# Four-term products of softmax weights and values per head, and earlier reads of weights, in a two-layer attention and expert trunk

## The chip, the cores and the metric

The kernel runs on one core of a Trainium2 chip. The metric is the device time of one execution in microseconds (us), from the runs that were timed; the profile is one further execution.

## The reference

The input is one sequence of 512 tokens of width 1024. Two layers follow each other, and each has a token mixer, a residual sum with layer norm, a feed-forward part of 16 experts of which each token uses two, and a second residual sum with layer norm.

```
for layer in range(2):
    mixed = mixer_dilated(x, ...) if layer == 0 else mixer_stick_breaking(x, ...)
    x = layer_norm(ALPHA * x + mixed, ln1_g[layer], ln1_b[layer])
    ffn = moe_ffn(x, router_w, router_b, exp_w_gate[layer], exp_w_up[layer], exp_w_down[layer])
    x = layer_norm(ALPHA * x + ffn, ln2_g[layer], ln2_b[layer])
```

The mixer of layer 0 projects three groups of queries, keys and values for 16 heads of 64; each group attends with a window and a dilation, `softmax(q k / 8 + bias) v`, and the groups are merged by their softmax denominators. The mixer of layer 1 is a stick-breaking attention with one group of queries, keys and values. All matrix products are wanted at fp32 accuracy.

## The kernel before, in words

**Splitting.** A number is carried as a high and a low part of type fp32r, `hi` (rounded by ACT, line 143) and `lo` (the remainder, by DVE, line 145); the helper is `split`. A product is three matmuls, hi·hi, hi·lo and lo·hi (`mm3`, lines 150 to 153). Weights come as chunks: `load` (line 205) fetches a chunk to `raw`, `split_to` makes `whi` and `wlo`, `weights` hands them out.

**Order.** The program is written as steps that are interleaved by hand (`interleave`, `beside`); a scheduler then orders the instructions of every engine by its own estimate. Each engine and each DMA queue works its list in order.

**Start.** The rows of x are loaded by SP (line 375), transposed by TensorE and split into `xT` (`rows_to_T`, line 324). Two of the four row blocks are transposed ahead of the first projection, the other two inside it (`rest`). `load_router` (line 390) loads the router's weights and the four rows of `ln1_g` and `ln1_b` from ACT's queue, the latter with one element per partition and run (line 400).

**Layer 0's attention** works in quarters of four heads. `project` makes Q, K and V of a unit; the far units (dilated, two groups together) and the near unit of a quarter are attended by `attend` (line 599). For each pair of heads `pr` and each half `b2` of the query blocks it takes a bank `po` from the pool `psD` (two banks), and for each of two blocks `j`: scores `S` (line 619), bias and row extreme on DVE (line 624), exponential on ACT (line 629), transposes (line 634), a split into `Ph` and `Pl` (line 637), and the product with the values, which are kept as `Vh` and `Vl` with the two heads of a pair side by side, 128 columns (line 639). A matmul there has the 128 columns of both heads against the 256 columns of both heads' weights, so half of what it makes is not used. ACT then copies each head's half to `acc` (line 642).

**Layer 1's weights, ahead.** Beside layer 0's projection steps, `split_ahead` (line 269) takes one quarter of a chunk of layer 1's weights: it loads it from HBM to a buffer `raw` (line 274), splits it, and stores the two parts to HBM (`kept`, line 276, POOL's queue). There are 64 such quarters. All use one buffer, which holds the raw quarter and both parts; the next load waits until the store before it has landed. Layer 1 then loads the parts by `parts_of` (line 278); each load is made to wait for the last expert load issued so far (`recent`) and for the last read of layer 0's sum (`read`). `prefetch` (line 900) starts the loads of the layer's first experts during the attention's end.

**Experts.** Each expert's output rows (96 slots, of which some are empty) are added to a DRAM tensor `x2_d` by an indirect DMA (line 1127). Empty slots go to spare rows behind the 512 tokens; those rows are filled first from `xres` (line 1286). At the end `post` sums each token's row: ACT copies both halves with an accumulated sum (line 1268), DVE makes the mean (line 1269), ACT the squares, DVE the scaled rows.

Of the kernel before, what the change touches and what calls it, by code (L numbers as in the profile page):

```python
# [70 lines left out]
def trunk_kernel(ctx, tc, A, out):  # L71
# [133 lines left out]
    def load(i):  # L205

        srcs, kind, j = chunks[i]
        if i in raws or kind == "b":
            return
        k = srcs[0].shape[1]  # L210
        if kind == "a":
            raw = rawp.tile([P, 2048], F32, name="raw0")
            raws[i] = [raw[:, :1024], raw[:, 1024:]]
            for half, t in enumerate(raws[i]):
                load_part(t, srcs, half, 2)
            return
# [155 lines left out]
    for n in range(4):  # L372
        if n == 2:
            load_to(1)
        sp.dma_start(xres[:, n, :], x[n * P:(n + 1) * P, :])

    rest = []
    for n in range(4):
        if n < 2:
            at["begun"] = rows_to_T(*xS, xres[:, n, :], n, streams=True)  # L380
        else:
            rest.append(lambda n=n: rows_to_T(*xS, xres[:, n, :], n, streams=True))
# [7 lines left out]
    def load_router():  # L390
        tmp = xp.tile([P, 5, KT * NE], F32, name="tmp", tag="Ol")
        rw = tmp[:, 0].rearrange("p (k e) -> p k e", k=KT)
        gbs = tmp[:, 1, :4 * KT].rearrange("p (j k) -> p j k", j=4)
        sums = tmp[:, 4, :4 * NE].rearrange("p (j e) -> p j e", j=4)
        with tc.issue_after(at["begun"]):
            act.dma_start(rw, A["router_w"].rearrange("(k p) e -> p k e", p=P))
            act.dma_start(rb, bass.AP(tensor=A["router_b"].tensor, offset=A["router_b"].offset, ap=[[0, P], [1, NE]]))
            for l in range(2):
                for i, name in enumerate(("ln1_g", "ln1_b")):
                    act.dma_start(gbs[:, 2 * l + i], A[name][l].rearrange("(k p) -> p k", p=P))  # L400
        for l in range(2):
            w2 = [rwg[l], tmp[:, 2].rearrange("p (k e) -> p k e", k=KT)]
            for i in range(2):
                tt(w2[i], rw, gbs[:, 2 * l + i, :, None].to_broadcast([P, KT, NE]), op=ALU.mult)
# [95 lines left out]
    def attention0(c, xSh, xSl, project_out):  # L500
# [50 lines left out]
        def project(far, u):  # L551
# [11 lines left out]
            def gen():  # L563
                for ct in range(2):
                    yield from project_T(xSh, xSl, [lambda ps: q_out(ct, ps), lambda ps: k_out(ct, ps)],
                                         "streams" if u == 0 and ct == 0 else None)
                    if ct == 0:
                        V.extend(qk.tile([P, 4, 256], F32R, name=f"V{s}") for s in "hl")
                        if far:
                            yield from project_V(xSh, xSl, *[lambda n2, t=t: t[:, n2 * 2:n2 * 2 + 2] for t in V])  # L570
                        else:
                            yield from project_V_near(V)
            def project_V_near(V):

                w = weights()
                for i in range(2):
                    ps, cs = bank(psA), slice(i * P, (i + 1) * P)
# [761 lines left out]
```

## Time and profile before

| | before |
|---|---|
| median of 3 runs | 1361.58 us (1356.65 to 1364.33) |
| the profiled execution: its time, its span | 1364.12 us, 1362.3 us |
| PE (TensorE) busy | 1247.7 us, 92% |
| weight loads of PE busy | 1022.9 us, 75% |
| DVE busy | 899.1 us, 66% |
| ACT busy | 859.0 us, 63% |
| POOL busy | 203.4 us, 15% |
| mean granted clock of TensorE | 0.954 of full speed |
| DMA | 289.60 MB, mean 213 GB/s |

The span is from the first to the last instruction; 1.8 us of the execution lie around it. A matmul's busy time overlaps that of the next, so the time that a matmul takes from the engine is read from the distance of two starts. The shares are means over stages: layer 0's attention lasts to about 618 us, its experts to about 830, layer 1's attention from about 875 to 1121, its experts to about 1325. A wait is named after what ended last before the instruction started; "issue" is idle time for which the profile shows no other engine.

### The profile page before, as it was taken

To read this page: it belongs to the slowest core of one execution; us is meant where nothing else is said; L and a number is where in the kernel's file an instruction comes from. 1 tells how busy PE (TensorE), PEld (TensorE's weight loads), DVE (VectorE), ACT (ScalarE), POOL (GpSimd) and SP (SyncE) were. 2 spreads that over 40 slices of the span, in tenths; PEclk is the share of its full clock that TensorE was granted. 3 is DMA by queue.
4 is the path that set the end of the run, shared out by engine and by line. 5 is a ranking of instruction groups with operands and counts; after the bars stand their busy time and mean duration, and the time that the engine had idled before them with its cause. 6 is when DMAs were issued, how large, how long until landed. Compare 5 with 4: busy or idle time off the path is not lost. (4 is left out here: it accounts for less than half of the span.)

```text
span 1362.3 us, 19699 instructions
## 1 busy us (share of the span) xinstructions
PE 1247.7 (92%) x6784; PEld 1022.9 (75%) x6784; DVE 899.1 (66%) x1620; ACT 859.0 (63%) x1538; POOL 203.4 (15%) x285
## 2 busy tenths in 40 slices
PE   6999999999999999988799987999999967899876
PEld 5998888789877879877577654988888856677543
DVE  4455665656555645576799774488878857798765
ACT  3356644665356635656699775387778756698664
POOL 3001000011001100010333110022221210332010
PEclk8999999999999999997799999999999977899997
DMA  8865455555455545478699996474444666799982
GB/s 239 284 216 171 155 186 167 178 166 171 147 186 171 164 149 174 158 255 309 226 299 320 312 291 239 132 215 154 156 155 155 218 234 213 249 318 316 288 261 106
DMA packets 176651, 289.60 MB, mean 213 GB/s; under 512 B 17787, under 2 KB 108027, under 8 KB 176540
## 3 DMA queue, kind: packets, MB, share of 16 engines
q1 hardware_dynamic: 153760, 230.72, 51.7%
q0 software_dynamic: 17344, 57.29, 13.5%
q8 instruction: 57, 0.93, 0.3%
q10 hardware_dynamic: 5436, 0.21, 0.3%
q14 instruction: 54, 0.44, 0.1%
HBM read 220.48 MB, written 63.50 MB: 208 GB/s over the span
## 5 line engine op out<-in xcount | busy, mean ns | idle before, releaser
L145 DVE TENSOR_TENSOR wlo<-raw,whi 128x1024 fp32r<-128x1024 f32 x176 | 212.8, 1221 | 94.8 <-ACT whi L143 93.4
L151 PE MATMUL bank<-xTh,whi 128*128 128x512 f32 (+1 forms) x608 | 235.3, 388 | 5.1 <-DVE kl L145 5.1
L152 PE MATMUL bank<-xTl,whi 128*128 128x512 f32 (+1 forms) x608 | 234.2, 385 | 0.0
L153 PE MATMUL bank<-xTh,wlo 128*128 128x512 f32 (+1 forms) x608 | 234.1, 385 | 0.0
L143 ACT ACTIVATE whi<-raw 128x1024 fp32r<-128x1024 f32 x176 | 183.7, 1054 | 67.4 <-PE bank L152 21.1
L145 DVE TENSOR_TENSOR raw<-raw 128x512 fp32r<-128x512 f32 x64 | 44.3, 692 | 141.7 <-ACT raw L143 141.7
L143 ACT ACTIVATE raw<-raw 128x512 fp32r<-128x512 f32 x64 | 40.4, 632 | 152.2 <-DMA raw<-sb_w_in 117.2
L151 PEld LDWEIGHTS bank<-xTh,whi 128*128 128x128 f32 x608 | 116.5, 192 | 24.5 <-issue 5.8
L153 PEld LDWEIGHTS bank<-xTh,wlo 128*128 128x128 f32 x608 | 116.5, 192 | 19.5
L152 PEld LDWEIGHTS bank<-xTl,whi 128*128 128x128 f32 x608 | 117.0, 192 | 18.2
L152 PE MATMUL bank<-wlo,XX 128*96 128x512 f32 x256 | 107.4, 420 | 7.3 <-DVE wlo L145 7.1
L151 PE MATMUL bank<-whi,XX 128*96 128x512 f32 x256 | 106.4, 416 | 7.1 <-ACT whi L143 7.0
L152 PE MATMUL bank<-wlo,xTh 128*128 128x256 f32 x384 | 109.3, 285 | 0.0
L151 PE MATMUL bank<-whi,xTh 128*128 128x256 f32 x384 | 109.1, 284 | 0.0
L153 PE MATMUL bank<-whi,xTl 128*128 128x256 f32 x384 | 109.1, 284 | 0.0
L276 POOL DMA_DIRECT2D kept<-raw x64 | 34.4, 537 | 478.1 <-DVE raw L145 448.5
L153 PE MATMUL bank<-whi,XX 128*96 128x512 f32 x256 | 104.1, 407 | 0.0
L1127 POOL DMA_INDIRECT x_d<-Y,wr x28 | 45.2, 1614 | 201.0 <-ACT Y L1124 139.5
L151 PEld LDWEIGHTS bank<-whi,xTh 128*128 128x128 f32 x384 | 73.7, 192 | 0.5 <-DVE xres L1273 0.2
L152 PEld LDWEIGHTS bank<-wlo,xTh 128*128 128x128 f32 x384 | 73.6, 192 | 0.5
L153 PEld LDWEIGHTS bank<-whi,xTl 128*128 128x128 f32 x384 | 73.3, 191 | 0.1
L629 ACT ACTIVATE Sb<-Sb,st 128x256 f32<-128x256 f32 (+1 forms) x128 | 61.6, 485 | 11.4 <-DVE st L624 11.2
(261 smaller groups left out, 2997.8 us busy)
## 6 DMA issues: line engine op xcount, KB each, us to landing
kept<-raw POOLq DMA_DIRECT2D x64, 512.0 KB, 3.1
raw<-dil_w_in SPq DMA_DIRECT2D x96, 256.0 KB, 4.5
raw<-exp_w_gate SPq DMA_DIRECT2D x32, 512.0 KB, 6.6
raw<-exp_w_up SPq DMA_DIRECT2D x32, 512.0 KB, 7.6
raw<-exp_w_down SPq DMA_DIRECT2D x16, 1024.0 KB, 8.4
whi<-kept SPq DMA_DIRECT2D x32, 512.0 KB, 5.8
wlo<-kept SPq DMA_DIRECT2D x32, 512.0 KB, 5.0
raw<-dil_w_in SPq DMA_DIRECT2D x24, 512.0 KB, 4.6
```

The source lines that it names most:

```text
L143: ins = act.activation(view(hi), src, AF.Copy, scale=scale).ins
L145: tt(view(lo), src, view(hi).bitcast(F32), op=ALU.subtract)
L151: pe.matmul(ps, lhsT=lh, rhs=rh, start=start, stop=False, **kw)
L152: pe.matmul(ps, lhsT=lh, rhs=rl, start=False, stop=False, **kw)
L153: pe.matmul(ps, lhsT=ll, rhs=rh, start=False, stop=stop, **kw)
L276: pool.dma_start(kept[i][part], raw[:, :1024].rearrange("p (j c) -> p j c", j=2))
L629: act.activation(sb[:, b0:, h, :], sb[:, b0:, h, :], AF.Exp, bias=st[:, n, hh, 0:1], scale=-1.0, accum_out=st[:, n, hh, 1:2])
L1127: pool.indirect_dma_start(out=x2_d[:, :], out_offset=bass.IndirectOffsetOnAxis(ap=row, axis=0), in_=Y, in_offset=None, compute_op=ALU.add)
```

## The change

1. **Values times weights (attend).** V of a unit is kept as one tile in which each head has its 64 high and 64 low columns side by side, and the softmax weights as `PP`, in which each head has 128 high and 128 low columns side by side. One matmul of 128 against 256 columns per head and key block makes all four products, lo·lo among them, which is not used. So there are two matmuls per key block and pair instead of three. Each head has a bank of its own, so a pair takes both banks of `psD`. ACT copies lo·hi to `acc`, and DVE adds hi·lo and hi·hi to it.
2. **Layer 1's weights.** One buffer stays allocated; it has two places for raw quarters. A quarter is loaded while the one before it is split. All loads of the parts wait for what the first of them waits for.
3. **Start.** The first chunk's halves are loaded between the row blocks of x. `ln1_g` and `ln1_b` come as 16 rows of 128 elements each and are transposed by TensorE.
4. **Experts.** Empty slots are dropped by a bounds check; the spare rows are gone.
5. **Closing layer norm.** The second half's sum is made by DVE.

```diff
@@ load, load_part
-    def load(i):
+    def load(i, halves=(0, 1)):
         srcs, kind, j = chunks[i]
-        if i in raws or kind == "b":
+        if kind == "b" or i in raws and 0 in halves:
             return
...
@@ split_ahead
     def split_ahead():
+        if not coming:
+            return
+        if "ahead" not in at:
+            at["ahead"] = rawp.tile([P, 2048], F32, name="raw1")
+            fetch_ahead()
+        raw = at["ahead"]
+        i, part = coming.pop(0)
+        src = raw[:, 1024 + part % 2 * 512:][:, :512]
+        fetch_ahead()
+        split(raw[:, :512].bitcast(F32R), raw[:, 512:1024].bitcast(F32R), src)
+        pool.dma_start(kept[i][part], raw[:, :1024].rearrange("p (j c) -> p j c", j=2))
+
+    def fetch_ahead():
         if coming:
-            i, part = coming.pop(0)
-            raw = rawp.tile([P, 2048], F32, name="raw1")
-            load_part(raw[:, 1024:1536], chunks[i][0], part, 4)
-            split(raw[:, :512].bitcast(F32R), raw[:, 512:1024].bitcast(F32R), raw[:, 1024:1536])
-            pool.dma_start(kept[i][part], raw[:, :1024].rearrange("p (j c) -> p j c", j=2))
+            i, part = coming[0]
+            with tc.issue_after(at["begun"]):
+                load_part(at["ahead"][:, 1024 + part % 2 * 512:][:, :512], chunks[i][0], part, 4)
@@ parts_of
-            for before in (at["recent"][-1], at["read"]):
+            at.setdefault("behind", (at["recent"][-1], at["read"]))
+            for before in at["behind"]:
                 after(ins, before)
@@ start
-        if n == 2:
-            load_to(1)
+        if n in (1, 2):
+            load(0, (n - 1,))
         sp.dma_start(xres[:, n, :], x[n * P:(n + 1) * P, :])
@@ load_router
-            for l in range(2):
-                for i, name in enumerate(("ln1_g", "ln1_b")):
-                    act.dma_start(gbs[:, 2 * l + i], A[name][l].rearrange("(k p) -> p k", p=P))
+            for i, name in enumerate(("ln1_g", "ln1_b")):
+                act.dma_start(rows[2 * KT * i:2 * KT * (i + 1)], A[name].rearrange("l (k p) -> (l k) p", p=P))
+        with tc.issue_after(at["begun"]):
+            gbs = bank(psC)[:, :4 * KT]
+            pe.transpose(gbs, rows, ident[:4 * KT, :4 * KT])
...
@@ attend
-                    po = bank(psD).rearrange("p (j h q) -> p j h q", j=2, h=2)
+                    po = [bank(psD).rearrange("p (j c q) -> p j c q", j=2, c=2) for _ in range(2)]
...
-                        Ph = sm.tile([P, 2, 2, P], F32R, name="Ph")
-                        Pl = sm.tile([P, 2, 2, P], F32R, name="Pl")
-                        split(Ph, Pl, pt[:, b0:], view=lambda t: t[:, b0:])
-                        for kb, (Q, K, (Vh, Vl)), kn in kbs:
-                            mm3(po[:, j], Vh[:, kn, vs], Vl[:, kn, vs], Ph[:, kb], Pl[:, kb], kb == b0, kb == 1)
+                        PP = sm.tile([P, 2, 2, 2, P], F32R, name="PP")
+                        split(PP[:, b0:, :, 0], PP[:, b0:, :, 1], pt[:, b0:])
+                        for h in range(2):
+                            for kb, (Q, K, (V,)), kn in kbs:
+                                pe.matmul(po[h][:, j].rearrange("p c q -> p (c q)"),
+                                          lhsT=V[:, kn, pr, 2 * h:2 * h + 2].rearrange("p s d -> p (s d)"),
+                                          rhs=PP[:, kb, h].rearrange("p c q -> p (c q)"), start=kb == b0, stop=kb == 1)
                     for h in range(2):
-                        s = slice(64 * h, 64 * h + 64)
-                        act.activation(perm(acc[s, pr, :], far)[:, 2 * b2:2 * b2 + 2, :], po[s, :, h, :], AF.Copy)
+                        s, other = slice(64 * h, 64 * h + 64), slice(64 - 64 * h, 128 - 64 * h)
+                        to = perm(acc[s, pr, :], far)[:, 2 * b2:2 * b2 + 2, :]
+                        act.activation(to, po[h][other, :, 0], AF.Copy)
+                        for c in (1, 0):
+                            tt(to, to, po[h][s, :, c], op=ALU.add)
@@ expert_down
-                                in_=Y, in_offset=None, compute_op=ALU.add)
+                                in_=Y, in_offset=None, compute_op=ALU.add, bounds_check=T - 1, oob_is_err=False)
@@ post
-                    for half, cs in enumerate(halves):
-                        act.activation(junk[:, cs], ps[half], AF.Copy, accum_out=st[:, n, half:half + 1])
+                    act.activation(junk[:, halves[0]], ps[0], AF.Copy, accum_out=st[:, n, 0:1])
+                    dve.tensor_reduce(st[:, n, 1:2], ps[1], axis=AX.X, op=ALU.add)
@@ layer
-        x2_d = dram.tile([T + P, D], F32, name=f"x2_d{l}")
-        sp.dma_start(x2_d[T:], xres[:, 0])
+        x2_d = dram.tile([T, D], F32, name=f"x2_d{l}")
```

Where instructions move, three places show it. The first is ACT's list at the program's start; `tmp<-ln_g` and `tmp<-ln_b` are DMAs that ACT issues, `xTh` the high part of x, and `raw_604` or `raw_602` the buffer of `split_ahead`. Before, and then with the change:

```order
L143 ACTIVATE xTh<-bank 128x16x32
L396 DMA tmp<-router_w 128x8x16
L397 DMA rb<-router_b 128x16
L400 DMA tmp<-ln_g 128x8x1
L143 ACTIVATE raw_604<-raw_604 128x512
L400 DMA tmp<-ln_b 128x8x1
L400 DMA tmp<-ln_g 128x8x1
L143 ACTIVATE whi<-raw_208 128x1024
L400 DMA tmp<-ln_b 128x8x1
L143 ACTIVATE xTh<-bank 128x16x32 x2
```

```order
L143 ACTIVATE xTh<-bank 128x16x32 x2
L415 DMA tmp<-router_w 128x8x16
L416 DMA rb<-router_b 128x16
L418 DMA tmp<-ln_g 16x128
L143 ACTIVATE raw_602<-raw_602 128x512
L418 DMA tmp<-ln_b 16x128
L143 ACTIVATE xTh<-bank 128x16x32 x2
```

Two DMAs of 1024 runs each and a split of weights no longer stand ahead of the two copies of `xTh` that end each list.

The second is PE's list at the first product of values and weights of a far unit, in the first quarter; rows of `xTh`, `xTl` are projections of the next unit, `Sb` rows are transposes. Before, and then with the change:

```order
L151 MATMUL bank<-xTh,whi 128x512
L151 MATMUL bank<-Ph,Vh 128x256
L152 MATMUL bank<-xTl,whi 128x512
L153 MATMUL bank<-xTh,wlo 128x512
L151 MATMUL bank<-xTh,whi 128x512
L152 MATMUL bank<-xTl,whi 128x512
L153 MATMUL bank<-xTh,wlo 128x512
L152 MATMUL bank<-Pl,Vh 128x256
L153 MATMUL bank<-Ph,Vl 128x256
L151 MATMUL bank<-Ph,Vh 128x256
L152 MATMUL bank<-Pl,Vh 128x256
L153 MATMUL bank<-Ph,Vl 128x256
```

```order
L151 MATMUL bank<-xTh,whi 128x512
L152 MATMUL bank<-xTl,whi 128x512
L153 MATMUL bank<-xTh,wlo 128x512
L664 MATMUL bank<-PP,V 128x256 x8
L659 MATMUL bank<-ident,Sb 128x128 x5
```

Of the twelve matmuls for the two blocks the first six are shown; there are eight now, and they stand together behind the projection.

The third is SP's list near the end of layer 1's attention; `kept_121` holds the parts of the last output weights, the rows of `exp_w` are the first expert loads. Before, and then with the change:

```order
L227 DMA rmh<-exp_w_down 128x2x1024
L227 DMA rmh<-exp_w_gate 128x1024
L227 DMA rmh<-exp_w_up 128x1024
L227 DMA rml<-exp_w_gate 128x1024
L227 DMA rml<-exp_w_up 128x1024
L227 DMA rml<-exp_w_down 128x2x1024
L281 DMA whi<-kept_121 128x2x512
L281 DMA wlo<-kept_121 128x2x512
```

```order
L294 DMA whi<-kept_121 128x2x512
L294 DMA wlo<-kept_121 128x2x512
L228 DMA raw_11423<-exp_w_gate 128x1024
L228 DMA raw_11423<-exp_w_up 128x1024
L228 DMA rmh<-exp_w_down 128x2x1024
L294 DMA whi<-kept_121 128x2x512
L294 DMA wlo<-kept_121 128x2x512
L228 DMA rmh<-exp_w_gate 128x1024
```

The first half of the parts moved ahead of all the expert loads, the second half ahead of all but three.

## Rows read from the trace of the kernel before


**Rows 1.** Busy time by stretch (us, engine busy, granted clock PEclk, DMA share, GB/s).

```profile
40.00:605.00 565.00, 545.44 (x3193) 474.32 (x3193) 317.24 (x661) 311.19 (x632) 48.93 (x88) 1.00 0.55 178
...
780.00:830.00 50.00, 41.45 (x158) 25.32 (x157) 35.35 (x48) 32.08 (x46) 4.48 (x4) 0.93 0.92 289
```

**Rows 2.** PE's waits from 40 to 605 us: engine, line, releaser, us, times, longest.

```profile
PE bank L151 <- ACT Ph L143: 6.6, 8, 1.6
PE bank L151 <- DVE kl L145: 5.1, 4, 3.0
PE bank L151 <- ACT kh L143: 4.8, 6, 1.1
```

**Rows 3.** PE in order of time, 28 to 31 us: start, us, engine, line.

```profile
28.28 1.97 PE L331 MATMUL bank<-ident,xres 128*128 128x128 f32 x8 [6.63 <-DVE xTl L145]
...
30.68 0.41 PE L151 MATMUL bank<-whi,xTh 128*128 128x256 f32 x1
30.89 0.41 PE L152 MATMUL bank<-wlo,xTh 128*128 128x256 f32 x1
```

**Rows 4.** ACT and its queue, 14 to 27 us, in order of time.

```profile
14.81 2.16 ACTq L400 DMA_DIRECT2D tmp<-ln_b  x1
...
22.71 1.06 ACT L143 ACTIVATE whi<-raw 128x1024 fp32r<-128x1024 f32 x1 [7.29 <-issue]
```

**Rows 5.** Busy time by stretch, two stretches with a lowered granted clock.

```profile
28.00:35.00 7.00, 6.72 (x32) 6.49 (x33) 4.87 (x11) 1.20 (x2) 0.00 (x0) 0.53 0.44 123
...
1094.00:1123.00 29.00, 17.82 (x55) 13.32 (x54) 14.11 (x25) 14.26 (x26) 3.79 (x7) 0.71 0.65 232
```

**Rows 6.** PE in order of time, 565 to 566 us; matmuls of 512 and 256 columns.

```profile
565.50 0.39 PE L153 MATMUL bank<-xTh,wlo 128*128 128x512 f32 x1
565.73 0.40 PE L151 MATMUL bank<-xTh,whi 128*128 128x512 f32 x1
...
566.20 0.28 PE L152 MATMUL bank<-Pl,Vh 128*128 128x256 f32 x1
566.32 0.28 PE L153 MATMUL bank<-Ph,Vl 128*128 128x256 f32 x1
```

**Rows 7.** Groups of instructions: count, busy us, mean ns, idle before.

```profile
L151 PE MATMUL bank<-Ph,Vh 128*128 128x256 f32 x120 | 34.9, 290 | 6.6 <-ACT Ph L143 6.6
...
L151 PEld LDWEIGHTS bank<-Ph,Vh 128*128 128x128 f32 x120 | 22.5, 188 | 11.0 <-ACT Ph L143 9.9
```

**Rows 8.** ACT's waits for the next layer's weight pieces, whole run.

```profile
ACT raw L143 <- DMA raw<-sb_w_in: 117.2, 44, 5.6
...
ACT raw L143 <- DMA raw<-sb_w_out: 35.0, 16, 4.7
```

**Rows 9.** One such piece on POOL, SP and ACT, in order of time.

```profile
490.24 0.53 POOL L276 DMA_DIRECT2D kept<-raw  x1 [6.93 <-DVE raw L145]
...
494.84 0.88 SPq L242 DMA_DIRECT2D raw<-sb_w_in  x2
...
497.62 0.63 ACT L143 ACTIVATE raw<-raw 128x512 fp32r<-128x512 f32 x1 [3.53 <-DMA raw<-sb_w_in]
```

**Rows 10.** SP's queue and PE near the second attention's last output weights.

```profile
1088.42 0.38 SPq L227 DMA_DIRECT2D rml<-exp_w_down  x1
...
1094.23 0.38 SPq L281 DMA_DIRECT2D whi<-kept  x1
...
1098.08 0.93 PE L151 MATMUL bank<-whi,Oh 128*128 128x512 f32 x3 [3.81 <-DMA whi<-kept]
```

**Rows 11.** DVE in order of time: contiguous and strided operands read from PSUM.

```profile
602.73 0.42 DVE L145 TENSOR_TENSOR Pl<-bank,Ph 128x256 fp32r<-128x256 f32 x1
...
561.54 1.09 DVE L145 TENSOR_TENSOR kl<-bank,kh 64x512 fp32r<-64x512 f32 x1 [0.42 <-ACT kh L143]
```

**Rows 12.** Groups of instructions: the experts' scatter-adds; the closing layer norm's first pass.

```profile
L1127 POOL DMA_INDIRECT x_d<-Y,wr x28 | 45.2, 1614 | 201.0 <-ACT Y L1124 139.5 <-ACT hh L143 22.5 <-ACT whi L143 15.3
...
L1268 ACT ACTIVATE junk<-bank 128x512 bf16<-128x512 f32 x16 | 9.4, 592 | 8.5 <-SPq L1241 4.3 <-PE bank L1261 4.2
```

More of the change, by code (lines that the diff above doesn't have):

```diff
@@ L211, in load @@
         if kind == "a":
[L212 to L215, printed above, removed]
+            if 0 in halves:
+                raw = rawp.tile([P, 2048], F32, name="raw0")
+                raws[i] = [raw[:, :1024], raw[:, 1024:]]
+            for half in halves:
+                load_part(raws[i][half], srcs, half, 2)
             return
@@ L372, in trunk_kernel @@
     for n in range(4):
-        if n == 2:
-            load_to(1)
+        if n in (1, 2):
+            load(0, (n - 1,))
         sp.dma_start(xres[:, n, :], x[n * P:(n + 1) * P, :])
+    at["load"] = 1
     rest = []
@@ L381, in trunk_kernel, with later @@
         else:
-            rest.append(lambda n=n: rows_to_T(*xS, xres[:, n, :], n, streams=True))
+            def later(n=n):
+                at["begun"] = rows_to_T(*xS, xres[:, n, :], n, streams=True)
+            rest.append(later)
+    first_rows = at["begun"]
     rb = const.tile([P, NE], F32, name="rb")
@@ L392, in load_router @@
         rw = tmp[:, 0].rearrange("p (k e) -> p k e", k=KT)
-        gbs = tmp[:, 1, :4 * KT].rearrange("p (j k) -> p j k", j=4)
+        rows = tmp[:4 * KT, 1]
         sums = tmp[:, 4, :4 * NE].rearrange("p (j e) -> p j e", j=4)
-        with tc.issue_after(at["begun"]):
+        with tc.issue_after(first_rows):
             act.dma_start(rw, A["router_w"].rearrange("(k p) e -> p k e", p=P))
             act.dma_start(rb, bass.AP(tensor=A["router_b"].tensor, offset=A["router_b"].offset, ap=[[0, P], [1, NE]]))
-            for l in range(2):
-                for i, name in enumerate(("ln1_g", "ln1_b")):
-                    act.dma_start(gbs[:, 2 * l + i], A[name][l].rearrange("(k p) -> p k", p=P))
+            for i, name in enumerate(("ln1_g", "ln1_b")):
[3 more added lines that the diff above has]
+            pe.transpose(gbs, rows, ident[:4 * KT, :4 * KT])
+        gbs = gbs.rearrange("p (i l k) -> p i l k", i=2, l=2)
         for l in range(2):
@@ L403, in load_router @@
             for i in range(2):
-                tt(w2[i], rw, gbs[:, 2 * l + i, :, None].to_broadcast([P, KT, NE]), op=ALU.mult)
+                tt(w2[i], rw, gbs[:, i, l, :, None].to_broadcast([P, KT, NE]), op=ALU.mult)
                 dve.tensor_reduce(sums[:, 2 * l + i], w2[i].rearrange("p k e -> p e k"), axis=AX.X, op=ALU.add)
@@ L567, in gen @@
                     if ct == 0:
-                        V.extend(qk.tile([P, 4, 256], F32R, name=f"V{s}") for s in "hl")
+                        V.append(qk.tile([P, 4, 2, 4, HD], F32R, name="V"))
                         if far:
-                            yield from project_V(xSh, xSl, *[lambda n2, t=t: t[:, n2 * 2:n2 * 2 + 2] for t in V])
+                            yield from project_V(xSh, xSl, *[
+                                lambda n2, s=s: V[0][:, n2 * 2:n2 * 2 + 2].rearrange("p n r s d -> p (n r) s d")[:, :, s]
+                                for s in (slice(0, 4, 3), slice(1, 3))])
                         else:
-                            yield from project_V_near(V)
+                            yield from project_V_near(V[0])
             def project_V_near(V):
@@ L576, in project_V_near @@
                 for i in range(2):
-                    ps, cs = bank(psA), slice(i * P, (i + 1) * P)
+                    ps = bank(psA)
                     for k in range(KT):
@@ L584, in project_V_near @@
                         pe.transpose(pt[:, n], VT[:, n * P:(n + 1) * P], ident)
-                    split(*V, pt, view=lambda t: t[:, :, cs])
+                    split(V[:, :, i, 0:4:3], V[:, :, i, 1:3], pt.rearrange("p n (s d) -> p n s d", s=2))
                     yield
@@ L602, in attend @@
             for pr in range(2):
-                vs = slice(pr * P, (pr + 1) * P)
                 for b2 in range(2):
-                    po = bank(psD).rearrange("p (j h q) -> p j h q", j=2, h=2)
+                    po = [bank(psD).rearrange("p (j c q) -> p j c q", j=2, c=2) for _ in range(2)]
                     for j in range(2):
```

## The prediction

> **What bounds the kernel now.** I read the table of busy time by stretch first, since each stage has limits of its own. In layer 0's attention PE is busy for 545.44 of 565 us at a granted clock of 1.00, while DVE and ACT work for 317.24 and 311.19 us and the DMA queues for 0.55 of the time [rows 1]: PE is the bound there, and DVE and ACT each have some 250 us to spare. In the expert stretch DMA takes over, at a share of 0.92 and 289 GB/s [rows 1]. Next comes the table of waits: PE's three largest in layer 0's attention are 6.6, 5.1 and 4.8 us, all for ACT or DVE [rows 2], together 16.5 us. Then the timelines of the two places where PE stands still for one reason. At the start a block of transposes at 28.28 us had waited 6.63 us for DVE's `xTl` [rows 3]. DVE was waiting for ACT, and ACT's gap of 7.29 us before 22.71 us has the releaser "issue" [rows 4]: its queue was issuing the loads of `ln1_g` and `ln1_b`, 2.16 us for the one shown [rows 4]. From 28 to 35 us the clock is then granted at 0.53 [rows 5], that is nearly all at 1.2 of 2.4 GHz, and two matmuls of 256 columns start 0.21 us apart [rows 3] where others take 0.12 [rows 6]. Near the end of the second attention PE waits 3.81 us for `whi<-kept` [rows 10], in a stretch whose clock is granted at 0.71 [rows 5].
>
> The sum below is made against the profiled execution, 1364.1 us, which is 2.5 above the median of the runs; the result is set 2.5 lower.
>
> **The start.** The loads stand behind the `xTh` copies in ACT's changed list, and the weights' split that stood there leaves it too. After the transposes a copy and a remainder still have to run. Such a pair costs 0.42 plus 1.09 us elsewhere [rows 11], so I leave PE 1.5 of the 6.63 us and take 5.1 off. If PE does not stand still, the stretch at 0.53 does too much waiting for 7 us: at full clock its work would need 0.53 of 7, or 3.7 us, and 3.3 us go. I take **-8** (bounds 0 and -10: nothing, if another load is late; gap and clock both gone). Half a weight chunk now comes ahead of x's second row block and half a chunk later than it did not; both are 0.5 MB, at 289 GB/s 1.8 us, one late by what the other is early: 0, bounds ±1.8. The added transpose on PE is one instruction, queued behind later row blocks, so its load has time: 0.
>
> **Values times weights.** The three lines of the old product have 120 matmuls each [rows 7]; two remain for each three, so 120 go. The spacing of two such matmuls is 0.12 us [rows 6], the columns stay 256, and PE is the bound: 120 x 0.12 = **-14** (bounds 0, if PE waits instead, and -14). By the matmuls' busy time it would be 34.9 us, and by the weight loads' 22.5 [rows 7], but both overlap their neighbours. The Trainium skill, Perfetto Trace Analysis, Identifying the Most-Contended Engine, calls the busy share of matmuls a bad measure of TensorE because they are pipelined, and recommends that of the weight loads. The rows agree on the first: 290 ns busy against a spacing of 120. They don't agree on the second here, since a load of 188 ns is also longer than the spacing; by that measure the term would be -22.5 and the sum 8.5 us lower.
>
> What it adds: 32 pairs and halves, each with four DVE additions of 64 x 256, or 128 in all, while the copies on ACT keep their number. A contiguous operation of 256 columns took 0.42 us, a strided one of 512 columns 1.09 [rows 11]. Half of the latter is about 0.55; I take 0.53 as the mean, 68 us (54 to 140 by the two rows), which lies in DVE's 250 us of slack. The bank `po` is the second matter: a pair now takes both banks of `psD`, so the first product of a pair waits until the last addition of the pair before. In PE's changed order some 20 projection matmuls of 512 columns stand between these, at 0.23 us each [rows 6], 4.6 us, against four additions of 2.1; only in the last quarter do a few transposes and output matmuls alone stand there. **+2** (bounds 0 and +10).
>
> **The read-ahead.** ACT waits 117.2 + 35.0 = 152.2 us for the raw quarters, in 60 waits of 2.5 us on average [rows 8]. In one piece the order is plain: POOL issues the store at 490.24, SP the next load at 494.84 when the store has landed, and ACT begins at 497.62 after a wait of 3.53 us [rows 9]. With two places the load is there; the split must still wait for the old store, since the parts have one place only. It could begin at 494.84, which leaves 0.75 of this wait and, over 60 waits, at most 45 of the 152.2 us. Behind a waiting split on ACT stand the copies of `Ph` and `kh`, and PE waits for these: 16.5 us [rows 2]. The same share, (152.2 - 45) / 152.2 = 0.70, gives **-12** (bounds 0 and -16.5). The traffic is unchanged, and DMA is at 0.55 there [rows 1].
>
> **Layer 1's parts.** The last output weights stand behind expert loads on SP's queue: `rml<-exp_w_down` is issued at 1088.42, `whi<-kept` at 1094.23 [rows 10]. In the changed list the first half is ahead of all of them, the second behind three. The 3.81 us go, and about 1.6 us of lowered clock behind them, an estimate as half of the idle time; **-5** (bounds 0 and -5.4). The expert loads move back by four loads of 0.5 MB, 7 us at 289 GB/s; they are wanted later than the output weights, which covers it.
>
> **Scatter.** 28 scatter-adds [rows 12], 14 per layer with 96 slots each, are 1344 slots per layer. The tokens' 1024 places less two experts at the mean of 64 are about 896. The 448 dropped rows of 4 KB are 1.8 MB, at 289 GB/s [rows 1] 6.3 us of DMA time per layer. PE is still busy for 41.45 of 50 us in that stretch, so most of it is hidden: **-3** (bounds 0 and -12). The spare rows' fill is 0.5 MB beside other work: 0.
>
> **Closing norm.** Eight of the 16 copies of 592 ns [rows 12] go to DVE, in pairs beside ACT's: 8 x 0.59 = -4.7 if all were on the path in the tail, +5 if DVE is slower by as much. DVE then must also make the mean behind its own sum; I take **0**.
>
> Sum: -8 - 14 + 2 - 12 - 5 - 3 = -40, so 1324.1 in the profile's terms and **1322** for the median. Its own range, with one of the middle terms halved or full, is 1311 to 1334.
>
> **Rivals.** *The waits of ACT were hidden, or only change their name.* For it speaks that PE waits 16.5 us where ACT waits 152; also the split stays tied to the store, so the read-ahead may not do what it says. Against it, the waits of 1 to 3 us in [rows 2] fit ACT being late. Read-ahead and scatter at 0: 1364.1 - 25 - 2.5 = 1337. Chance 0.20.
>
> *PE's saving is given back.* The scores, row extremes and exponentials between two products are a chain over four engines; where it sets the pace, PE has nothing to gain from fewer matmuls, and the additions lengthen it. Against it speaks PE's 545 of 565 us. Products at 0 and the additions at +8: -20, or 1342. Chance 0.12.
>
> *All terms at their good ends,* -10 - 14 - 16.5 - 5.4 - 12 = -58: 1304. Chance 0.11.
>
> *Slower: the loss of the second bank.* If the scheduler's projections are not there when wanted, each of the 31 passages from one pair's products to the next makes PE wait for four additions, 2.1 us, or 66 in all, and the forecast's -40 becomes +26: 1388. It decides from where less than 2.1 us of PE work, nine matmuls of 0.23, stand between the pairs. The changed order has about 20 nearly everywhere, which speaks against it. The Trainium skill, Perfetto Trace Analysis, Optimizing Tensor Performance, says that independent groups of matmuls should rotate through different banks so that the evacuation of one overlaps the next; the change gives this rotation up. The rows of before, with two banks in rotation, cannot show what that costs. Chance 0.04.
>
> **How the numbers follow.** The forecast has 0.50, the rivals 0.20, 0.12, 0.11 and 0.04; 0.03 is left for small effects that cancel (no change). The range of 1308 to 1344 holds the forecast and the first two rivals; it leaves out half of the good ends' case and more, the slow one, and tails of the others, 2 in 10. A measurement of this kernel can tell about 0.5%, or 6.8 us, from no change: under 1354.8 is faster, above 1368.4 slower. All but the slow case and the cancelled one lie under it; with a little from the second rival's far end, 0.91 faster, 0.05 the same, 0.04 slower.
>
> **What would show it.** In the new profile: no "issue" gap of 7 us on ACT near 20 us, PE's gap there under 2, and a granted clock near 1.00 from 28 to 35; 240 products, still 0.12 apart; ACT's waits for `raw` from 152 to under 45, and PE's waits for `Ph`, `kl` and `kh` to about 5; no wait of PE for an addition beyond 1 us; no wait for `whi<-kept`; DVE's busy time up by some 68 us less a little. The prediction is wrong if PE's waits for `Ph` or the additions grow past 20 us, if the start keeps its gap, or if DMA makes PE wait longer in the experts.

## The result, and the profile after

The changed kernel takes 1317.04 us (median of 4 runs, 1313.12 to 1319.65) against 1359.12 us of the kernel before in the same comparison: ratio 0.9687, interval 0.9638 to 0.9736. That is 42 us less, where 40 had been forecast. The profiled execution has a span of 1317.4 us.

First the page's busy times (us, share of the span, instructions):

```profile
PE 1220.6 (93%) x6665; PEld 1005.0 (76%) x6665; DVE 967.8 (73%) x1756; ACT 859.2 (65%) x1522; POOL 199.2 (15%) x285
```

PE has 27 us less to do and DVE 69 us more; ACT has as much as before. Where the time went is read from the starts of the same instructions in both traces. In their names `kh` and `kl` are the high and low part of K, `Sb` the scores with their bias, `rX` the router's input, `XX` the inputs of an expert and `Yh` the high part of the outputs of a layer's last two experts:

| stage (from, to) | before, us | after, us | difference |
|---|---|---|---|
| start, to ACT's first copy of K | 39.4 | 30.1 | -9.3 |
| attention of layer 0, to its last product of values and weights | 576.7 | 547.2 | -29.5 |
| output, norm and router, to the first expert's `XX` | 44.2 | 43.3 | -0.9 |
| experts, to the first `Yh` | 161.6 | 159.9 | -1.7 |
| closing norm, to the first keys of layer 1 | 52.3 | 56.6 | +4.3 |
| attention of layer 1, to the router's first copy of `rX` | 255.3 | 249.5 | -5.8 |
| router, experts, closing norm, end | 232.8 | 230.8 | -2.0 |

The stage of the closing norm scatters from kernel to kernel: it takes 50.3 to 57.6 us in the kernels below that keep the old norm and 52.7 to 59.6 in those with the new one, so the +4.3 is not read as an effect of the edit.

**The start.** ACT's timeline from 13 to 18 us (start, us, engine or its queue):

```profile
13.87 0.47 ACTq L418 DMA_DIRECT2D tmp<-ln_g  x1
...
14.41 0.41 ACTq L418 DMA_DIRECT2D tmp<-ln_b  x1
...
17.65 1.09 ACT L143 ACTIVATE xTh<-bank 128x512 fp32r<-128x512 f32 x2 [2.63 <-PE bank L346]
```

A load's issue takes 0.41 to 0.47 us in place of 2.16 [rows 4], and ACT now waits for PE. PE's longest wait between 12 and 40 us is 1.1 us, where it was 6.63 [rows 3]. Of the 9.3 us of the table 6.6 are left at the first product of values and weights (89.2 us in place of 95.8).

Busy time by stretch (us, busy of PE, PEld, DVE, ACT, POOL, granted clock, DMA share, GB/s):

```profile
28.00:35.00 7.00, 7.00 (x61) 7.00 (x60) 4.52 (x5) 3.79 (x5) 0.35 (x1) 1.00 1.06 383
40.00:567.00 527.00, 517.85 (x3007) 453.05 (x3006) 372.17 (x773) 313.16 (x626) 48.32 (x86) 1.00 0.59 189
...
1057.00:1080.00 23.00, 15.91 (x55) 12.13 (x54) 14.23 (x25) 14.17 (x26) 3.79 (x7) 0.72 0.69 234
```

From 28 to 35 us 61 matmuls run at full clock where 32 ran at 0.53 [rows 5]. In the attention PE is busy for 98% in place of 97, and DVE for 71% in place of 56 [rows 1].

PE's longest waits from 31 to 567.5 us, then ACT's waits for layer 0's weights and for the quarters, over the whole run (us, times, longest):

```profile
PE bank L151 <- ACT kh L143: 2.8, 4, 1.4
PE bank L659 <- ACT Sb L654: 2.1, 2, 1.6
PE bank L152 <- DVE kl L145: 2.0, 6, 0.6
PE bank L664 <- DVE acc L672: 1.1, 3, 0.5
```

```profile
ACT whi L143 <- DMA raw<-dil_w_in: 38.3, 19, 4.5
...
ACT raw L143 <- DMA kept<-raw: 26.5, 12, 6.1
ACT raw L143 <- issue: 17.2, 12, 3.2
```

Of the waits of 6.6, 5.1 and 4.8 us [rows 2] the first is gone, and `kl` and `kh` are down to 2.0 and 2.8. No wait for a quarter's load is left of the 152.2 us [rows 8]. Part of it has changed its name: ACT now waits 26.5 us for the store, and 38.3 us for layer 0's own weights, where it was 7.1 before. At the products the additions make PE wait for 1.1 us, and once more for 1.2 at a projection of the attention's output.

Products and stores before, then products, additions and stores with the change, as groups by line (ns min/median/max, first and last start in us):

```profile
L151 PE MATMUL bank<-Ph,Vh x120: 276/280/388, 95.8 to 615.8; 128*128 128x256 f32 x120
L153 PE MATMUL bank<-Ph,Vl x120: 276/280/285, 97.2 to 616.1; 128*128 128x256 f32 x120
L276 POOL DMA_DIRECT2D kept<-raw x64: 532/532/765, 16.5 to 594.6; - x64
```

```profile
L664 PE MATMUL bank<-PP,V x240: 276/281/368, 89.2 to 577.3; 128*128 128x256 f32 x120
```

```profile
L672 DVE TENSOR_TENSOR acc<-acc,bank x128: 401/526/641, 92.2 to 579.1; 64x256 f32<-64x256 f32 x128
```

```profile
L283 POOL DMA_DIRECT2D kept<-raw x64: 532/532/765, 16.1 to 466.2; - x64
```

The first and the last product lie 488.1 us apart; before they lay 520.3 apart (95.8 to 616.1). The last of the 64 stores is issued at 466.2 us; before, at 594.6 (the first at 16.1 and 16.5). A piece, which is one quarter's load, split and store, takes (466.2 - 16.1) / 63 = 7.1 us on average in place of 9.2. This pair of numbers carries what follows.

### The profile page after: what moved, and what is told of

Same layout as the page of the kernel before. It is cut to its first block, busy times and chain, and to the rows that moved or that the text cites. A ratio compares the mean times of both kernels' runs of the same rounds, so it can differ in the third digit from the quotient of the medians.

```text
span 1317.4 us, 19542 instructions
## 1 busy us (share of the span) xinstructions
PE 1220.6 (93%) x6665; PEld 1005.0 (76%) x6665; DVE 967.8 (73%) x1756; ACT 859.2 (65%) x1522; POOL 199.2 (15%) x285
## 5 line engine op out<-in xcount | busy, mean ns | idle before, releaser
L143 ACT ACTIVATE whi<-raw 128x1024 fp32r<-128x1024 f32 x176 | 183.6, 1054 | 92.3 <-DMA raw<-dil_w_in 38.3
L151 PE MATMUL bank<-whi,XX 128*96 128x512 f32 x256 | 104.2, 407 | 7.3 <-ACT whi L143 7.0
L152 PE MATMUL bank<-wlo,XX 128*96 128x512 f32 x256 | 104.5, 408 | 6.4 <-DVE wlo L145 6.2
L153 PE MATMUL bank<-whi,XX 128*96 128x512 f32 x256 | 101.7, 397 | 0.0
L143 ACT ACTIVATE raw<-raw 128x512 fp32r<-128x512 f32 x64 | 40.3, 629 | 68.8 <-DMA kept<-raw 26.5
L672 DVE TENSOR_TENSOR acc<-acc,bank 64x256 f32<-64x256 f32 x128 | 66.1, 516 | 6.5 <-ACT acc L670 4.1
```

What stands on the lines that cost most here:

```text
L143: ins = act.activation(view(hi), src, AF.Copy, scale=scale).ins
L151: pe.matmul(ps, lhsT=lh, rhs=rh, start=start, stop=False, **kw)
L152: pe.matmul(ps, lhsT=lh, rhs=rl, start=False, stop=False, **kw)
L153: pe.matmul(ps, lhsT=ll, rhs=rh, start=False, stop=stop, **kw)
L672: tt(to, to, po[h][s, :, c], op=ALU.add)
```

## The experiments

Times stand beside the kernel before in the same comparison (its median 1358 to 1361 us), with ratio and interval. "Products' span" is the time from the first to the last product of values and weights. An edit also lets the scheduler order the lists anew, which was not held fixed.

### One part alone

Each of these is the kernel before with one part of the change, whose diff stands above.

```diff
 kernel before
+ attend, project, project_V_near: V and PP with parts side by side, a bank per head
```

> The kernel before with the new products alone (one matmul per head and key block, 240 in place of 360, four DVE additions per pair). Own theory: PE is the bound of layer 0's attention, so 120 x 0.12 = 14 us of PE work go and at most 2 come back: 11 to 14 us less than the kernel before, and PE's waits in layer 0's attention stay near 17 us, since ACT still waits about 150 us for the raw quarters. Rival 'saving given back': the chain of scores sets the pace; less than 4 us of gain, and PE's waits there grow by about 10 us. Rival 'second bank lost': some 50 us slower, with waits of PE for the DVE additions of about 60 us.

Measured: 1389.30 us, ratio 1.0221 (1.0146 to 1.0297), **slower** by 29 us. The second-bank rival is not the reason at the products: there PE waits 0.2 us for the additions between 40 and 625 us. One wait of 8.5 us carries their name, at a projection of the attention's output, and it comes from a late quarter:

```profile
617.49 0.63 ACT L143 ACTIVATE raw<-raw 128x512 fp32r<-128x512 f32 x1 [7.81 <-DMA raw<-sb_w_out]
618.15 0.78 ACT L648 ACTIVATE acc<-bank 64x256 f32<-64x256 f32 x2
...
620.22 0.77 PE L151 MATMUL bank<-whi,Oh 128*128 128x512 f32 x1 [8.51 <-DVE acc L650]
```

ACT stood 7.8 us for the quarter; the last pair's copies come behind that split, the additions behind the copies, and PE waits for these. Products, stores and SP's queue:

```profile
L642 PE MATMUL bank<-PP,V x240: 276/281/552, 97.2 to 611.0; 128*128 128x256 f32 x120
```

```profile
L276 POOL DMA_DIRECT2D kept<-raw x64: 532/532/769, 17.1 to 636.5; - x64
```

```profile
597.56 0.67 SPq L227 DMA_DIRECT2D rml<-exp_w_up  x1
598.50 10.30 SPq L242 DMA_DIRECT2D raw<-sb_w_out  x2
611.30 0.33 SPq L227 DMA_DIRECT2D Y<-exp_w_gate  x1
...
622.27 0.33 SPq L242 DMA_DIRECT2D raw<-sb_w_out  x1
639.41 0.33 SPq L940 DMA_DIRECT2D x_d<-xres  x1
```

The products' span shrank by 6.5 us only (513.8), and the last store is at 636.5 us, 25 us behind the last product; a piece takes 9.8 us on average. The last quarters' loads, each waiting for the store before it, now stand among the first expert loads on SP's queue. At the router's first matmul 9 expert loads had been issued in place of 16. From the last product to the first `XX` it takes 55.8 us in place of 44.3, with the 8.5 us wait in it, and from there to the first `Yh` 178.9 in place of 161.6. That second stretch (busy time as above), first of this kernel, then of the kernel before:

```profile
667.00:846.00 179.00, 156.54 (x719) 105.33 (x717) 135.77 (x165) 130.80 (x186) 38.92 (x26) 0.97 0.96 299
660.00:822.00 162.00, 153.97 (x720) 105.84 (x719) 132.36 (x163) 128.54 (x184) 39.07 (x29) 0.96 0.97 300
```

The rate is the same, the DMA share is near 1 in both, and 179 us at 299 GB/s are 53.5 MB in place of 48.6: the 4.9 MB more, 16 us at that rate, fit what the stretch lost. PE waited for

```profile
PE bank L151 <- ACT whi L143: 8.9, 9, 1.7
PE bank L152 <- DVE wlo L145: 8.5, 18, 0.8
```

there (before: 3.4 and 3.3 us).

```diff
 kernel before
+ split_ahead, fetch_ahead: two places for raw quarters
```

> The kernel before with the read-ahead of layer 1's quarters alone. Own theory: ACT is late at times because it stands waiting for a quarter, and PE then waits for Ph, kh and kl; with ACT's waits for raw from 152 to under 80 us (of any name), PE's waits between 40 and 605 us fall from about 18 us to under 8, and the time by 10 to 16 us. Rival 'ACT's waits were hidden': ACT's waits fall in the same way, and the time by less than 4 us.

Measured: 1345.55 us, ratio 0.9895 (0.9863 to 0.9928), 14 us less; the products' span is 504.4 us, 15.9 less. PE's waits between 40 and 600 us are 9.2 in all, a little over the 8 expected. Of them:

```profile
PE bank L151 <- ACT kh L143: 3.1, 3, 2.1
...
PE bank L151 <- ACT Ph L143: 0.3, 1, 0.3
```

So ACT's waits were not hidden, as a whole; how the gain splits is shown with the square below.

```diff
 kernel before
+ start, load, load_router: halves between x's row blocks, ln1 as 16 rows
```

> The kernel before with the new start alone (first chunk's halves between the row blocks of x, ln1_g and ln1_b as 16 rows each). Own theory: ACT's gap of 7.29 us goes and with it PE's wait of 6.63 us and the stretch at half clock: 7 to 10 us less, all of it won before 40 us and none lost later. Rival 'another load is late': ACT's issue gap goes, but PE waits for x or for the first weights; under 4 us.

Measured: 1355.72 us, ratio 0.9965 (0.9932 to 0.9999): 5 us, with an interval from nothing to 9. At ACT's first copy of K its profile is 6.2 us ahead, a little less than expected; PE's longest wait between 12 and 40 us is under 1 us.

```diff
 kernel before
-            for before in (at["recent"][-1], at["read"]):
+            at.setdefault("behind", (at["recent"][-1], at["read"]))
+            for before in at["behind"]:
```

> The kernel before with the new rule for the loads of layer 1's parts alone. Own theory: the wait of 3.81 us for whi<-kept goes, and some lowered clock with it: 4 to 6 us less, all won between 1090 and 1125 us. Rival 'given back': the expert loads that now come later make PE wait at the start of layer 1's experts for as much: within 2 us of the kernel before.

Measured: 1352.84 us, ratio 0.9938 (0.9901 to 0.9975): 8 us (3 to 13). Between 1080 and 1105 us of the kernel before it wins 5.8 us; the rest lies in the experts, whose stretches vary by as much (last section).

The four parts alone add up to 29 - 14 - 5 - 8 = +2 us. Together, with the experts' and the norm's edits, they gave -42. So at least two of them depend on each other.

### Which two, and why

The changed kernel with one part undone:

```diff
 changed kernel
- split_ahead, fetch_ahead: two places for raw quarters
+ split_ahead as before: one place
```

> The changed kernel with the old reading of layer 1's quarters (one place, load behind the store). Theory 'chain of pieces': with one place the 64 pieces are a chain of load, split and store of some 9 us each, as long as layer 0's attention itself; with the quicker products the last pieces fall behind it, four of them between the first expert loads on SP's queue, and the expert loads come some 35 us late, which the experts' DMA-bound end pays. So this kernel loses the read-ahead's and the products' gain: 30 to 50 us over the changed kernel's 1317, 1347 to 1367, with the last store of a piece later than the end of the attention's products. Rival 'the parts add up': the read-ahead is worth the 14 us that it gave alone; about 1331.

Measured: 1372.47 us, ratio 1.0096 (1.0067 to 1.0126): 55 us slower than the changed kernel, more than the theory's 50, and slower than the kernel before.

```profile
L652 PE MATMUL bank<-PP,V x240: 276/281/552, 89.3 to 606.1; 128*128 128x256 f32 x120
```

```profile
L277 POOL DMA_DIRECT2D kept<-raw x64: 532/532/765, 16.4 to 631.9; - x64
```

The stores again end 26 us behind the products, 9 expert loads have been issued at the router's first matmul (18 in the changed kernel), and the experts take 178.2 us. The parts don't add up; the chain theory holds here, and its size was put a little too low.

```diff
 changed kernel
- V and PP with parts side by side, a bank per head
+ three matmuls per key block, one bank per pair, copies by ACT
```

> The changed kernel with the old products of weights and values (three matmuls, one bank per pair, no DVE additions). Theory 'chain of pieces': with the chain out of the way the products are worth what PE saves, 120 x 0.12 = 14 us less at most 2: 1329 to 1334, and the difference grows evenly over layer 0's attention. Rival 'the products cost by themselves' (additions, banks), as their run alone would say: this kernel is 15 to 29 us faster than the changed one, 1288 to 1302.

Measured: 1326.02 us, ratio 0.9738 (0.9690 to 0.9786): 9 us over the changed kernel (7 by the ratios, whose intervals overlap, so that the whole time alone does not show a gain), below the expected window and far from the rival's. The products' span is 504.4 us (87.9 to 592.3) against 488.1, so the products save 16.3 us in place. Of these, 8 are lost again in this pair of profiles in the second layer's experts, 161.6 against 153.5 us, which no edit of the pair touches.

```diff
 kernel before
+ split_ahead, fetch_ahead: two places for raw quarters
+ V and PP with parts side by side, a bank per head
```

> The kernel before with the read-ahead and the new products, nothing else: the fourth corner of a square whose others are 1361 (neither), 1389 (products alone) and 1346 (read-ahead alone). Theory 'ACT's chain of pieces is a second bound': with the chain gone the products are worth what PE saves, so layer 0's attention from the first product to the last takes some 488 us, 16 less than with the read-ahead alone, and the whole 1328 to 1335. Rival 'no interaction, the products cost': 1360 to 1375.

Measured: 1334.73 us, ratio 0.9839 (0.9815 to 0.9863); products' span 490.0 us:

```profile
L654 PE MATMUL bank<-PP,V x240: 276/281/367, 98.1 to 588.1; 128*128 128x256 f32 x120
```

The square is complete: without the read-ahead the products make the kernel 29 us slower, with it 11 us faster (1345.55 to 1334.73; 8 by the ratios), 14.4 in their span. The products' spans of its four corners (busy time as above): before, products alone, read-ahead alone, both.

```profile
95.80:616.10 520.30, 500.74 (x2916) 433.55 (x2915) 298.31 (x633) 291.38 (x597) 46.23 (x83) 1.00 0.53 173
97.20:611.00 513.80, 488.72 (x2787) 422.36 (x2785) 355.23 (x755) 291.83 (x594) 44.49 (x81) 0.99 0.51 166
95.50:599.90 504.40, 495.00 (x2916) 434.52 (x2915) 297.11 (x631) 293.20 (x597) 45.65 (x81) 1.00 0.55 177
98.10:588.10 490.00, 480.66 (x2785) 419.74 (x2784) 356.83 (x755) 294.77 (x594) 45.69 (x81) 0.99 0.57 182
```

PE's idle time, the span less PE's busy time, is 19.6, 25.1, 9.4 and 9.3 us. With the read-ahead the products take 14.3 us of work off PE, and nothing comes back as idle time; without it they take 12.0 off, and 5.5 come back. The read-ahead alone saves 10.2 us of idle time and 5.7 of busy time with as many matmuls; for the latter no run gives the reason.

Is it the number of pieces in the chain? Two kernels with 56 loads and splits (the stores stay 64), the second with the new products:

```diff
             pool.dma_start(kept[i][part], raw[:, :1024].rearrange("p (j c) -> p j c", j=2))
+            if part == 2 and list(kept).index(i) % 2:
+                coming.pop(0)
+                pool.dma_start(kept[i][3], raw[:, :1024].rearrange("p (j c) -> p j c", j=2))
```

> The kernel before with 56 pieces in the same way (some of layer 1's weights are other weights), as the base of the run with the new products. Theory 'chain of pieces': a little shorter, by the PE waits that eight pieces fewer cause: 1352 to 1361. Rival 'the pieces do not matter': as before, 1358 to 1364.

> The kernel before with the new products, and 56 pieces in place of 64: for every second chunk the last quarter of the parts is not loaded and split, the third quarter's parts are stored in its place too (so some of layer 1's weights are other weights). Theory 'chain of pieces': the chain of 56 ends before the attention does, the expert loads are not held up, and the 20 us that the new products alone lost in layer 0's experts are not lost: 25 to 40 us less than the products alone with 64 pieces (1389), 1349 to 1364; compared with 56 pieces and the old products 8 to 14 us less. Rival 'additions and banks': the number of pieces matters little, over 1375.

Measured: 1353.67 us (0.9964, 0.9941 to 0.9987) and 1355.82 us (0.9958, 0.9930 to 0.9986). By the ratios, eight pieces fewer are worth 5 us with the old products and 36 with the new (1.0221 to 0.9958, of 1360). The loss is gone: the stores end at 560.7 us, ahead of the last product at 614.8, 18 expert loads have been issued at the router's first matmul, and the experts take 157.2 us. But nothing is gained either, where 8 to 14 us were expected, and a piece now takes 9.6 and 9.9 us, so the chain has no fixed time per piece. PE's waits from 40 to 600 us without and with the new products:

```profile
PE bank L151 <- DVE kl L145: 5.7, 4, 3.9
PE bank L151 <- ACT kh L143: 2.7, 3, 1.2
```

```profile
PE bank L151 <- ACT kh L143: 9.3, 7, 3.9
PE bank L151 <- DVE kl L145: 5.5, 7, 1.6
PE bank L640 <- ACT Sb L635: 4.0, 7, 1.6
PE bank L645 <- DVE acc L653: 3.6, 6, 1.2
```

The products' spans are 517.2 and 518.8 us: what PE saved came back as idle time (16.7 us in the first, 28.2 in the second). ACT stands at each quarter until it has landed (92.0 + 35.8 us in the second kernel), and `kh` and the exponentials of `Sb` stand behind it in ACT's list. That ACT's place in this chain is what takes the gain, and not DVE's additions, was not tried apart here; the square above, where the same additions cost nothing once the chain is loose, speaks for it.

### The additions, the places, the ends

```diff
-                        act.activation(to, po[h][other, :, 0], AF.Copy)
-                        for c in (1, 0):
-                            tt(to, to, po[h][s, :, c], op=ALU.add)
+                        for again in range(2):
+                            act.activation(to, po[h][other, :, 0], AF.Copy)
+                            for c in (1, 0):
+                                tt(to, to, po[h][s, :, c], op=ALU.add)
```

> The changed kernel with the taking-over of the products done twice (copy and both additions, then the same copy and additions again; the result is the same). Both banks are held some 6.2 us per pair in place of 3.1 (two copies of 0.50 and four additions of 0.52, twice), 66 us more on DVE and 32 on ACT. Theory 'cover': PE has about 4.6 us of projections between two pairs' products, so the first 3.1 us cost nothing and of the second a part shows: 10 to 40 us slower, with PE's waits for the additions up from 1.1 us to over 8. Rival 'the banks never matter': under 6 us slower, and PE's waits for the additions stay under 3 us.

Measured: 1358.74 us, ratio 0.9993 (0.9975 to 1.0012), 42 us slower than the changed kernel. PE's waits from 40 to 600 us:

```profile
PE bank L151 <- ACT kh L143: 9.1, 8, 2.0
PE bank L152 <- DVE kl L145: 4.1, 4, 1.5
...
PE bank L664 <- DVE acc L673: 1.5, 1, 1.5
```

Neither theory foresaw this. The price is just above the first one's window, but it is not paid at the banks: PE waits 1.5 us for the additions. The products' spans of the changed kernel and of this one:

```profile
89.20:577.30 488.10, 478.95 (x2784) 418.42 (x2783) 356.36 (x754) 294.04 (x594) 45.66 (x81) 1.00 0.57 183
89.60:611.20 521.60, 494.11 (x2788) 425.89 (x2787) 419.89 (x878) 326.62 (x657) 47.98 (x81) 0.98 0.54 171
```

Of the 33.5 us between them 18.3 are idle time of PE, with late `kh` and `kl` first among its waits, and 15.2 are busy time of as many matmuls, at a granted clock of 0.98 in place of 1.00. So 96 us more on DVE and ACT stretch the span by 33.5 us, while the change's own 66 us of additions (128 x 0.516) cost none that shows in the square. The slack that DVE's mean share promises is not there at every moment.

```diff
-        src = raw[:, 1024 + part % 2 * 512:][:, :512]
+        to = raw[:, part % 2 * 1024:][:, :1024]
         fetch_ahead()
-        split(raw[:, :512].bitcast(F32R), raw[:, 512:1024].bitcast(F32R), src)
-        pool.dma_start(kept[i][part], raw[:, :1024].rearrange("p (j c) -> p j c", j=2))
+        split(to[:, :512].bitcast(F32R), to[:, 512:].bitcast(F32R), to[:, 512:])
+        pool.dma_start(kept[i][part], to.rearrange("p (j c) -> p j c", j=2))
...
-                load_part(at["ahead"][:, 1024 + part % 2 * 512:][:, :512], chunks[i][0], part, 4)
+                load_part(at["ahead"][:, part % 2 * 1024 + 512:][:, :512], chunks[i][0], part, 4)
```

> The changed kernel with two places for the parts as well: the low part is written over its raw quarter, so the split no longer waits for the store of the piece before, and a load waits for the store of the piece before that. ACT's waits of 26.5 us for kept<-raw should go. Theory 'what is left is hidden': PE's waits in layer 0's attention are only about 9 us by now, so 0 to 5 us less. Rival 'ACT is still a bound': 8 to 15 us less. Other side: the load waits for a store again, and ACT for the load; up to 5 us more.

Measured: 1343.88 us, ratio 0.9906 (0.9883 to 0.9930), 27 us **slower** than the changed kernel; none of the three sizes was right. ACT's waits from 40 to 600 us, a stretch of SP's queue, and the stores:

```profile
ACT raw L143 <- DMA raw<-sb_w_in: 70.1, 33, 6.4
ACT whi L143 <- DMA raw<-dil_w_in: 38.6, 13, 9.7
ACT raw L143 <- DMA raw<-sb_w_out: 29.1, 13, 5.8
```

```profile
307.68 12.30 SPq L243 DMA_DIRECT2D raw<-sb_w_in  x6
320.08 2.05 SPq L243 DMA_DIRECT2D raw<-dil_w_in  x4
```

```profile
L283 POOL DMA_DIRECT2D kept<-raw x64: 532/532/765, 16.4 to 380.2; - x64
```

The products' span is 521.3 us in place of 488.1. The wait for the store left ACT and went to SP. The scheduler now orders the pieces closer, one every (380.2 - 16.4) / 63 = 5.8 us; the loads wait for stores, six issues take 12.3 us of SP's queue, layer 0's own weights stand behind them (ACT's longest wait for these is 9.7 us), and ACT again waits 99.2 us for quarters. The "other side" of the expectation had the right mechanism and a fifth of its size. What the closer order costs by itself, without the waiting loads, was not tried.

```diff
 changed kernel
- scatter with bounds check; second half's sum by DVE
+ spare rows, filled first; both sums by ACT
```

> The changed kernel with the old scatter-add (empty slots to spare rows, which are filled first) and the old closing layer norm (both halves' sums by ACT). Prediction's terms: the scatter 3 us and the norm 0, so 3 us slower than the changed kernel, of which the stretches of the experts would show 1 to 2 each. Rival 'both hidden': within 2 us. Bound of the prediction: 12 us.

Measured: 1310.54 us, ratio 0.9658 (0.9637 to 0.9680), the lowest time of all kernels here. Its interval overlaps that of the changed kernel (0.9638 to 0.9736), so whether the two ends cost anything is open; that they gain 3 us is not borne out. Expert stretches of 159.2 and 160.8 us stand against 159.9 and 161.6.

## Why the prediction was right, and the step of it that failed

- **Start, -8.** 9.3 us at the first copy of K and 6.6 at the first product; alone 6.2 at the copy and 5 in the time. Gap and clock went as said; right in size or a little high. The 1.5 us left to PE were read from two remainders on DVE [rows 11], where a copy and a remainder were meant; 1.1 were left.
- **Products, -14 + 2.** In the changed kernel 16.3 us by the products' span with and without them (14.4 in the square), the additions at 0.516 us (0.53 assumed) and PE's wait for them 1.1 us. Right in size, but the step that failed stands here: "PE is the bound" was taken as a property of the stage, with bounds of 0 and -14 for the products and 0 and +10 for the additions, whatever stands beside them. Alone they cost 29 us. PE was busy 97% [rows 1] *and* the chain of pieces lasted from 16.5 to 594.6 us, as long as the stage; a second bound just under the first. With fewer matmuls and the old chain PE stood idle for ACT, and the last pieces fell among the expert loads. The rival "PE's saving is given back" had this right in kind, for another chain, and gave it a chance of its own instead of a condition: whether the read-ahead is in.
- **Read-ahead, -12.** 14 us alone, 15.9 in the products' span. The forecast priced PE's waits alone, and of these about 10 us went; the other 5.7 were not in its sum, so the total is in part luck. Its second effect was not seen: without it the change would have been 55 us slower.
- **Parts, -5.** 5.8 us in place. Right in size. The first half of the parts is issued at 1036.52 us, ahead of all the expert loads, the second at 1039.82, behind three, and the wait for `whi<-kept` [rows 10] is gone. The matmul that had waited comes 4.0 us earlier against those before it; that the rest is a lowered clock is not shown, since the stretch that follows still has 0.72 where it had 0.71 [rows 5].
- **Scatter, -3.** Not found; the step that failed is "most of it is hidden": all of it is, or less than can be read.
- **Norm, 0.** Nothing that can be told from the scatter of its stage.
- **The second bank (slower).** Not what happened. The Trainium skill (Perfetto Trace Analysis, Optimizing Tensor Performance) asks that independent groups rotate through banks; here giving it up cost 1.1 us of waits at the products, up to 3.6 in the other kernels with the new products, and holding both banks twice as long left it at 1.5. That the projections between two pairs cover it, as the prediction argued, fits this and was not tried apart.
- **The measure of PE.** 14.4 to 16.3 us for 120 matmuls, or 120 to 136 ns each, is near the spacing of 0.12 us [rows 6], not the 22.5 us of the loads' busy time [rows 7]. The Trainium skill (Perfetto Trace Analysis, Identifying the Most-Contended Engine) recommends the weight loads' busy share for judging how close TensorE is to its roofline; for the price of this edit it would have misled, and the measurement decides.

That the total came out within 5 us is in part luck. It rests on the parts being there together: the same sum, made for the products alone, says -12, and measured were +29. And errors cancelled: the attention of layer 0 gained more than products and read-ahead were given, and the scatter's 3 us were not found.

## What to carry to other kernels

Before costing an edit on the busiest engine, multiply out every chain that runs beside the stage (here 64 pieces of 9.2 us against an attention of 577 us): one just under the bound takes the saving, and what it still has to do falls into the next stage. The product of count and time is only a first look: with 56 pieces the chain ended 54 us ahead of the products, the loss was gone, and the saving was still taken. An engine that stands waiting in order for a transfer belongs to such a chain even when its own busy share is 55%. And a load that has to wait for a store should not stand on a queue ahead of loads that somebody needs, as the kernel with two places for the parts suggests.

## What the runs showed of the hardware that was not expected

The second layer's experts are the same code in all these kernels but for the scatter-add (in the two kernels with 56 pieces some weights ahead of them differ), and their time still differs: from the first `XX` to the first `Yh` 165.0 us in the profile of the kernel before, between 153.5 and 162.9 in the others. No cause was looked for. A term of 3 us in such a stretch, like the scatter's, cannot be read from one profile of each kernel.
